# Shifting the stationary split weights by 64 bytes in their buffers

## The chip, the cores and the metric

The kernel runs on one core of a Trainium2 chip. The metric is the device time of one execution in microseconds (us); the kernel before took 1667.27 us as the median of three executions (1665.71 to 1668.77).

## The reference

Two transformer-like blocks run one after the other on 256 tokens of width 1024, all in 32-bit floats. The first has a gated feed-forward layer, a mixer (a chunked mLSTM and a spatial gating unit) and a second feed-forward layer. The second block has two rounds of feed-forward, mixer (a pooled state-space layer in the first round, latent attention in the second), feed-forward, each modulated by vectors computed from `c`. Nearly all of the work is products of the tokens with large weight matrices, above all the six feed-forward layers:

```python
def swiglu(x, w_in, w_out):
    gate, up = jnp.split(x @ w_in, 2, axis=-1)     # w_in: 1024 x 5632
    return (jax.nn.silu(gate) * up) @ w_out        # w_out: 2816 x 1024
```

## The kernel before

Every large product is computed in three passes of a fast 32-bit mode (the type `F32R`). An operand `a` is split into `hi`, its rounded value, and `lo = a - hi`; `mm3` (L503 to L507) then adds `hi*hi`, `hi*lo` and `lo*hi` into the same PSUM tile, one matmul on each of the lines L505, L506 and L507. A matmul has a stationary operand of 128 columns, which a weight load puts into the array first, and a moving operand that streams through it column by column.

The weights arrive from HBM in 1 MB pieces (`raw`), packed in the order of use. A piece holds two units. `_split_one` (L333) turns one unit, 128 partitions by up to 1024 numbers, into a buffer `[P, 2, D]` with `hi` in its first and `lo` in its second half: ScalarE writes `hi` (L352), VectorE writes `lo` (L353). Six such buffers (`sp`) rotate, and between stages up to six working slots (`sx`) are lent to the same purpose; in one stage a pair of other tiles serves (`sg`). `pump` splits ahead as buffers come free, `take` hands out the next unit, `free` gives its buffer back one step later. The order of all units is fixed in the plans at the top of the file (`STAGES`).

A unit is a tuple; the sixth entry of a `cols` unit is the number of 128-row blocks in it. It is 8 for units made by `_mtile` (128 output columns, all of the 1024 input rows) and 2 for units made by `_chunk`. The two kinds are used differently:

- Units with 8 are stationary. `chan_chunk` (L875, chunks 2 to 10 of each feed-forward layer) and `m_tile` (L953, in the two mixers `mix` and `ssd`) take `hi[:, k*128:(k+1)*128]` as the stationary operand and `xh[:, k]` or `xl[:, k]`, the 256 tokens of one 128-row block of the split activations, as the moving one. Each unit makes 8 x 3 = 24 matmuls of 256 columns. There are 6 x 9 x 4 = 216 such units in the feed-forward layers, 16 in `mix` and 12 in `ssd`.
- All other units are moving: 128 tokens of split activations (`xh`, `xl`, `hT` and others) are stationary, and 512 columns (in `mla` also 384 or 288) of `hi` or `lo` stream past them.

`skinny` (L961) makes two small projections whose split weights lie in a tile of their own, `skw`, with 8 (`mix`) or 16 (`ssd`) columns for each 128-row block. There the stationary operand has only those 8 or 16 columns, and the moving one is again `xh[:, k]` or `xl[:, k]`.

The change moves tiles. Within a partition the program before puts the scratch area for DMA descriptors at byte 0 (16384 bytes), `skw` at 25408, `maskb` at 29888, the six `sp` buffers at 54976 and every 8192 bytes after, the eight slots from 104128 on (slots 2 and 5 are 8448 bytes long, the others 8192), and `xh` and `xl` at 170176 and 178368. A 128-column block of a split unit is 512 bytes, a block of `xh` 1024 bytes. So `sp`, all slots, `xh` and `xl` start at the same place in 128 bytes and in 256 bytes; in 512 bytes, slots 3 to 5 start 256 bytes away from the others.

Of the kernel before, what the change touches and what calls it, by code (L numbers as in the profile page):

```python
# [8 lines left out]
F32R = mybir.dt.float32r  # L9
# [4 lines left out]
P = 128  # L14
D = 1024
# [5 lines left out]
LN_EPS = 1e-5  # L21
ROPE_THETA = 10000.0
NEG = -1.0e30

# [88 lines left out]
def _size(u):  # L115
    return D if u[0] == "rows" else u[5] * sum(b - a for a, b in u[3])
# [94 lines left out]
def constants():  # L211
    ident = np.eye(P, dtype=np.float32)
    tri = np.triu(np.ones((P, P), np.float32))
    neg = np.triu(np.full((P, P), NEG, np.float32), 1)
    inv = (ROPE_THETA ** (-np.arange(0, 32, 2, dtype=np.float64) / 32)).astype(np.float32)
# [13 lines left out]
class Builder:  # L229
# [103 lines left out]
    def _split_one(self):  # L333
        u = self.next_split
        gi, base, last = self.group_of[u]
        while self.next_raw <= gi:
            self._load_raw()
        n = _size(self.units[u])
        src = self.raws[gi][:, base:base + n]
        if self.main_free:  # L340
            self.main_free -= 1
            self.where[u] = None
            t = self.p_split.tile([P, 2, D], F32R, tag="sp", name="sp")
        else:
            w = self.extra_free.pop(0)
            self.where[u] = w
            t = self.slot(w, [P, 2, D], F32R, "sx") if w < 8 else None
        if t is None:
            hi, lo = (self.p_gate.tile([P, D], F32R, tag="gate", name="sg") for _ in range(2))
        else:  # L350
            hi, lo = t[:, 0], t[:, 1]
        self.nc.scalar.activation(out=hi[:, 0:n], in_=src, func=AF.Copy)  # L352
        self.nc.vector.tensor_tensor(out=lo[:, 0:n], in0=src, in1=hi[:, 0:n], op=ALU.subtract)  # L353
        self.ready[u] = (hi, lo)
        self.next_split += 1
        if last:
            del self.raws[gi]
            while self.next_raw < len(self.offs) and len(self.raws) < self.RAW_BUFS:
                self._load_raw()
# [1505 lines left out]
```

## Time and profile before

| | |
|---|---|
| median of three executions | 1667.27 us |
| the profiled execution's own time | 1665.83 us |
| its span, first to last instruction | 1664.0 us |
| TensorE matmuls, busy | 1627.7 us (98%), 10290 instructions |
| VectorE, busy | 1180.4 us (71%) |
| ScalarE, busy | 820.9 us (49%) |
| DMA, mean | 219 GB/s |

The profile is of one execution. Its engines are PE (TensorE's matmuls), PEld (its weight loads, which run beside matmuls), DVE (VectorE), ACT (ScalarE), POOL (GpSimd) and SP (the queue that issues most DMAs). A matmul's time in the profile runs from its start to the modelled end of its last result, and matmuls overlap; how fast they follow each other is read from the difference of two starts in the timeline.

### The profile page before, as it was taken

How to read it: one execution, taken by the hardware profiler on the slowest of the kernel's cores; microseconds unless marked ns; L12 is line 12 of the kernel's file. 1: busy time of each engine (PE TensorE's matmuls, PEld its weight loads, DVE VectorE, ACT ScalarE, POOL GpSimd, SP SyncE). 2: the span in 40 equal slices, each digit the busy share in tenths (PEclk: the TensorE clock that was granted, in tenths of full speed). 3: DMA queues.
4: the chain of work that ended last, by engine and by line, in shares of the span. 5: the costliest groups of instructions: out<-in, count | busy, mean ns of one | idle time of the engine just before them, and what ended most of it. 6: DMA issues, size and time to landing. Idle time of an engine off the chain costs nothing.

```text
span 1664.0 us, 25287 instructions
## 1 busy us (share of the span) xinstructions
PE 1627.7 (98%) x10290; PEld 1462.1 (88%) x10290; DVE 1180.4 (71%) x1729; ACT 820.9 (49%) x1161; POOL 53.1 (3%) x81
## 2 busy tenths in 40 slices
PE   8999999999999999999999999999999999999997
PEld 6999889888799988999898789998999987889997
DVE  6698578796687867777586777766777576676553
ACT  6544465445554446444465464444544366555442
POOL 0000001100000000000004000000000010000000
PEclk9999999999999999999999999999999999999999
DMA  8788354676588745887344269873788444147640
GB/s 315 263 326 326 124 189 148 231 251 213 199 301 285 288 154 220 313 296 284 108 150 148 101 253 335 289 285 117 283 298 289 144 166 152 52 177 255 226 164 26
DMA packets 62469, 363.80 MB, mean 219 GB/s; under 512 B 7056, under 2 KB 7184, under 8 KB 28944
## 3 DMA queue, kind: packets, MB, share of 16 engines
q1 hardware_dynamic: 62208, 362.10, 60.3%
q8 instruction: 81, 1.33, 0.3%
q14 instruction: 36, 0.29, 0.1%
q10 hardware_dynamic: 144, 0.08, 0.0%
HBM read 361.11 MB, written 1.05 MB: 218 GB/s over the span
## 4 chain that ended last, share of the span: by engine, by line
PE 89%; DVE 5%; ACT 4%; DMA 1%; issue 1%; POOL 0%; POOLq 0%; SPq 0%; ACTq 0%; DVEq 0%
PE tp L506 14%; PE tp L507 14%; PE tp L505 14%; PE mm L505 7%; PE mm L507 7%; PE mm L506 7%; PE mm L690 7%; PE mm L691 7%; PE mm L697 7%; DVE sp L353 2%; DMA raw<-in_wts 1%; ACT sp L352 1%; ACT xn L635 1%; PE tp L618 1%; ACT xn L586 1%
## 5 line engine op out<-in xcount | busy, mean ns | idle before, releaser
L353 DVE TENSOR_TENSOR sp<-raw,sp 128x1024 fp32r<-128x1024 f32 (+2 forms) x375 | 453.5, 1220 | 224.8 <-ACT sp L352 224.4
L352 ACT ACTIVATE sp<-raw 128x1024 fp32r<-128x1024 f32 (+2 forms) x375 | 389.7, 1050 | 388.9 <-PE tp L507 212.2
L505 PE MATMUL tp<-xh,sp 128*128 128x256 f32 x1032 | 292.5, 283 | 0.2 <-ACT gate L463 0.2
L506 PE MATMUL tp<-xl,sp 128*128 128x256 f32 x1032 | 292.0, 283 | 0.0
L507 PE MATMUL tp<-xh,sp 128*128 128x256 f32 x1032 | 292.0, 283 | 0.0
L353 DVE TENSOR_TENSOR sx<-raw,sx 128x1024 fp32r<-128x1024 f32 x161 | 196.2, 1221 | 97.2 <-ACT sx L352 96.8
L352 ACT ACTIVATE sx<-raw 128x1024 fp32r<-128x1024 f32 x161 | 169.3, 1054 | 177.6 <-PE tp L507 125.7
L505 PEld LDWEIGHTS tp<-xh,sp 128*128 128x128 f32 x1032 | 198.0, 192 | 1.4 <-ACT gate L463 0.5
L506 PEld LDWEIGHTS tp<-xl,sp 128*128 128x128 f32 x1032 | 198.0, 192 | 0.9
L505 PE MATMUL tp<-xh,sx 128*128 128x256 f32 x696 | 197.2, 283 | 0.8 <-ACT gate L463 0.8
L507 PEld LDWEIGHTS tp<-xh,sp 128*128 128x128 f32 x1032 | 198.0, 192 | 0.0
L507 PE MATMUL tp<-xh,sx 128*128 128x256 f32 x696 | 196.9, 283 | 0.0
L506 PE MATMUL tp<-xl,sx 128*128 128x256 f32 x696 | 196.9, 283 | 0.0
L427 DVE SCALAR_TENSOR_TENSOR mraw<-mraw,c_act 128x1024 f32<-128x1024 f32 x144 | 175.3, 1218 | 0.0
L505 PEld LDWEIGHTS tp<-xh,sx 128*128 128x128 f32 x696 | 133.5, 192 | 1.9 <-ACT gate L463 1.0
L505 PE MATMUL mm<-sp,xh 128*128 128x512 f32 (+2 forms) x340 | 133.0, 391 | 1.8 <-ACT xh L639 1.8
L506 PEld LDWEIGHTS tp<-xl,sx 128*128 128x128 f32 x696 | 133.5, 192 | 0.9
L507 PEld LDWEIGHTS tp<-xh,sx 128*128 128x128 f32 x696 | 133.5, 192 | 0.0
L507 PE MATMUL mm<-sp,xl 128*128 128x512 f32 (+2 forms) x340 | 130.0, 382 | 0.2
L506 PE MATMUL mm<-sp,xh 128*128 128x512 f32 (+2 forms) x340 | 129.5, 381 | 0.0
L690 PE MATMUL mm<-sp,hT 128*128 128x512 f32 x246 | 96.6, 393 | 2.6 <-ACT hT L864 2.0
L691 PE MATMUL mm<-sp,hT 128*128 128x512 f32 x246 | 96.2, 391 | 0.0
(472 smaller groups left out, 2796.0 us busy)
## 6 DMA issues: line engine op xcount, KB each, us to landing
raw<-in_wts SPq DMA_DIRECT2D x260, 1024.0 KB, 5.2
mraw<-in_mod SPq DMA_DIRECT2D x144, 512.0 KB, 5.5
raw<-in_wts SPq DMA_DIRECT2D x4, 768.0 KB, 4.5
raw<-in_wts SPq DMA_DIRECT2D x5, 512.0 KB, 5.1
row<-in_rows SPq DMA_DIRECT2D x3, 512.0 KB, 6.3
raw<-in_wts SPq DMA_DIRECT2D x2, 576.0 KB, 4.1
rows<-in_rows SPq DMA_DIRECT2D x2, 512.0 KB, 6.4
bp<-in_pool SPq DMA_DIRECT2D x1, 1024.0 KB, 7.7
```

The lines of the kernel that those rows point to most:

```text
L352: self.nc.scalar.activation(out=hi[:, 0:n], in_=src, func=AF.Copy)
L353: self.nc.vector.tensor_tensor(out=lo[:, 0:n], in0=src, in1=hi[:, 0:n], op=ALU.subtract)
L427: nc.vector.scalar_tensor_tensor(out=src, in0=src, scalar=1.0, in1=self.c_act, op0=ALU.mult, op1=ALU.mult, accum_out=acc[:, kt:kt + 1])
L505: nc.tensor.matmul(out, ah, bh, start=first, stop=False)
L506: nc.tensor.matmul(out, ah, bl, start=False, stop=False)
L507: nc.tensor.matmul(out, al, bh, start=False, stop=last)
L586: nc.scalar.activation(out=xn[:, sl], in_=x[:, sl], func=AF.Square, scale=1.0 / 32.0, accum_out=ss[:, h:h + 1])
L618: nc.tensor.transpose(ps[:, j, :], src[:, k * P:(k + 1) * P], self.ident)
L635: nc.scalar.activation(out=vb[1][:, j], in_=banks[1][:, j], func=AF.Identity, scale=g[:, 4 + j:5 + j], bias=sh[:, 4 + j:5 + j])
L690: nc.tensor.matmul(accs[t][h], ah, hi[:, sl], start=(k == 0), stop=False)
L691: nc.tensor.matmul(accs[t][h], ah, lo[:, sl], start=False, stop=False)
L697: nc.tensor.matmul(accs[t][h], al, hi[:, sl], start=False, stop=False)
```

## The change

A split buffer becomes `[P, 2, D + 64]`, 256 bytes longer in each half, 8704 bytes in all. Units with 8 blocks, the stationary ones, are written and read 16 numbers (64 bytes) further into each half; all other units stay at the start of each half. The second half (`lo`) of every unit starts 4352 bytes after the first instead of 4096. The slots 3, 4, 6 and 7 grow by 512 bytes, 2 and 5 by 256. The scratch area for DMA descriptors that the program reserves goes from 16384 to 2048 bytes, and everything behind it moves down.

```diff
+DP = D + 64
+SHIFT = 16
...
-            t = self.p_split.tile([P, 2, D], F32R, tag="sp", name="sp")
+            t = self.p_split.tile([P, 2, DP], F32R, tag="sp", name="sp")
...
-            t = self.slot(w, [P, 2, D], F32R, "sx") if w < 8 else None
+            t = self.slot(w, [P, 2, DP], F32R, "sx") if w < 8 else None
...
-            hi, lo = t[:, 0], t[:, 1]
+            o = SHIFT if self.units[u][0] == "cols" and self.units[u][5] == 8 else 0
+            hi, lo = t[:, 0, o:o + D], t[:, 1, o:o + D]
...
-    nc = bacc.Bacc("TRN2", target_bir_lowering=False, num_devices=1)
+    nc = bacc.Bacc("TRN2", target_bir_lowering=False, num_devices=1, dynamic_dma_scratch_size=2048)
```

## Rows read from the trace of the kernel before

**Rows 1.** The page: span, busy time of the engines, granted clock and DMA in 40 slices.

```profile
span 1664.0 us, 25287 instructions
...
PE 1627.7 (98%) x10290; PEld 1462.1 (88%) x10290; DVE 1180.4 (71%) x1729; ACT 820.9 (49%) x1161; POOL 53.1 (3%) x81
...
PEclk9999999999999999999999999999999999999999
...
GB/s 315 263 326 326 124 189 148 231 251 213 199 301 285 288 154 220 313 296 284 108 150 148 101 253 335 289 285 117 283 298 289 144 166 152 52 177 255 226 164 26
```

**Rows 2.** The page: the chain that ended last, by engine.

```profile
PE 89%; DVE 5%; ACT 4%; DMA 1%; issue 1%; POOL 0%; POOLq 0%; SPq 0%; ACTq 0%; DVEq 0%
```

**Rows 3.** Groups by line and shape, TensorE: count, busy us, mean ns, idle before.

```profile
L505 PE MATMUL tp<-xh,sp 128*128 128x256 f32 x1032 | 292.5, 283 | 0.2 <-ACT gate L463 0.2
...
L505 PE MATMUL tp<-xh,sx 128*128 128x256 f32 x696 | 197.2, 283 | 0.8 <-ACT gate L463 0.8
...
L505 PE MATMUL mm<-xh,sp 128*128 128x256 f32 x224 | 64.8, 289 | 0.0
```

**Rows 4.** TensorE's timeline, first feed-forward layer, one chunk: start us, us, instruction.

```profile
58.27 0.28 PE L505 MATMUL tp<-xh,sp 128*128 128x256 f32 x1
58.38 0.28 PE L506 MATMUL tp<-xl,sp 128*128 128x256 f32 x1
...
69.78 0.40 PE L690 MATMUL mm<-sx,hT 128*128 128x512 f32 x1
...
75.25 0.28 PE L505 MATMUL tp<-xh,sp 128*128 128x256 f32 x1
```

**Rows 5.** TensorE's timeline, the projection with 8 stationary columns.

```profile
215.50 0.28 PE L505 MATMUL tp<-xh,skw 128*8 128x256 f32 x1
...
217.02 0.28 PE L506 MATMUL tp<-xl,skw 128*8 128x256 f32 x1
...
217.49 0.28 PE L507 MATMUL tp<-xh,skw 128*8 128x256 f32 x1
...
218.28 0.40 PE L505 MATMUL mm<-sp,xh 128*128 128x512 f32 x1
```

**Rows 6.** TensorE's timeline, the projection with 16 stationary columns.

```profile
827.18 0.28 PE L505 MATMUL tp<-xh,skw 128*16 128x256 f32 x1
...
829.99 0.28 PE L505 MATMUL mm<-xh,sp 128*128 128x256 f32 x1
```

**Rows 7.** TensorE's timeline, 288 moving columns of a split unit.

```profile
1359.54 0.29 PE L505 MATMUL mm<-sp,xh 128*128 128x288 f32 x1
...
1359.94 0.30 PE L505 MATMUL mm<-sp,xh 128*128 128x288 f32 x1
...
1360.34 0.29 PE L505 MATMUL mm<-sp,xh 128*128 128x288 f32 x1
```

**Rows 8.** TensorE's timeline, plain 32-bit matmuls and the 512-column ones behind them.

```profile
300.00 1.02 PE L1071 MATMUL tp<-qT,kT 128*128 128x256 f32 x4
300.86 0.61 PE L1073 MATMUL tp<-qT,kT 128*128 128x128 f32 x4
...
301.54 0.40 PE L506 MATMUL mm<-sp,xh 128*128 128x512 f32 x1
...
302.47 0.39 PE L507 MATMUL mm<-sp,xl 128*128 128x512 f32 x1
```

**Rows 9.** TensorE's timeline, the first matmuls after a stall.

```profile
173.72 0.28 PE L506 MATMUL tp<-xl,sx 128*128 128x256 f32 x1
...
174.78 0.28 PE L506 MATMUL tp<-xl,sx 128*128 128x256 f32 x1
```

**Rows 10.** Busy time by window, first feed-forward layer: engines, granted clock, DMA share, GB/s.

```profile
40.00:174.00 134.00, 133.19 (x957) 126.09 (x956) 107.05 (x133) 62.42 (x70) 0.00 (x0) 1.00 0.83 307
```

**Rows 11.** The page's groups, ScalarE's half of the split: busy, mean ns, idle before, releaser.

```profile
L352 ACT ACTIVATE sp<-raw 128x1024 fp32r<-128x1024 f32 (+2 forms) x375 | 389.7, 1050 | 388.9 <-PE tp L507 212.2
...
L352 ACT ACTIVATE sx<-raw 128x1024 fp32r<-128x1024 f32 x161 | 169.3, 1054 | 177.6 <-PE tp L507 125.7
```

## The prediction

> **What bounds the kernel now.** I read the page first: TensorE is busy for 1627.7 of 1664.0 us, at a granted clock of 9 or more tenths in every slice, the 2.4 GHz level [rows 1]. The chain that ended last agrees, 89% of it TensorE [rows 2]. The other engines follow: the ScalarE half of the split spends its idle time waiting for TensorE's matmuls of line L507 to give a buffer back [rows 11], not the other way round. So time is won or lost in the pace of matmuls, and a cheaper VectorE or DMA would bring nothing.
>
> Next, the groups by shape. The matmuls that the change shifts are those with `sp` or `sx` as stationary and 256 columns of `xh` or `xl` as moving operand. Line L505 alone has 1032 + 696 + 224 = 1952 of them [rows 3]; L506 and L507 have as many each, in all 5856, which is also what the plans give (244 units x 24). Their mean of 283 ns is start to end and says nothing of the pace, so I took the pace from the timeline. In one chunk of the first feed-forward layer, 96 of them run from 58.27 to 69.78 us, 11.51 us or 119.9 ns each [rows 4]. At 2.4 GHz 256 columns are 106.7 ns, so each carries 13.2 ns, 32 columns' worth, beyond its stream. Over 5856 that is 77 us, 4.6% of the span: all that the change can possibly win there.
>
> **The change part by part.** *No instruction is added or removed.* The splits keep their shapes, the DMAs their sizes and order. The writes of a split land elsewhere. ScalarE's split takes 1050 ns into `sp` and 1054 ns into `sx` [rows 11], tiles at quite different addresses, so I cost the moved writes at nothing. If they did grow by a tenth, the cover would be the waiting on TensorE in the same rows: 388.9 us before 389.7 us of work on ScalarE.
>
> *The DMA scratch.* 14336 bytes go, and 6 x 512 + 2560 = 5632 bytes are needed. All packets that carry weights are issued from SP in the kernel's code. I cost the smaller area at nothing; the cover, if it delayed descriptors, is the prefetch of three raw pieces. It would show first in the first feed-forward layer, which already moves 307 GB/s [rows 10].
>
> *The address arithmetic.* Everything behind the scratch moves by 14336 and then by 5632 bytes, both multiples of 256. So in 256 bytes all tiles keep their places, and the one new thing is that 5856 matmuls have their stationary operand 64 bytes away from the place of their moving one. Besides, the `lo` halves move by 256 bytes; that this is harmless is shown by `sx`: three of its slots already lie 256 bytes away from `sp`, and their group has the same 283 ns as that of `sp` [rows 3]. A shift by 128 bytes is in the trace too: with 288 moving columns every second block starts 1152 bytes on, 128 beyond a multiple of 256, and one block after the other takes the same 0.40 us for three [rows 7], 133.3 ns each or again 32 columns over the 288. So 128 and 256 bytes make no difference; if an offset matters at all it does so in 128 bytes, where 64 is as far from the present state as one can go.
>
> *What a matmul pays for.* Four rows bracket it. Plain 32-bit matmuls with 256 columns follow each other in 0.86 us / 4 = 215 ns [rows 8]; if I read the doubled pace as two passes of 106.7 ns, about 2 ns are left, so a matmul with a full stationary operand need not carry 13 ns. With only 8 stationary columns against the same moving tile the pace is 1.52 us / 13 = 116.9 ns at first and 0.79 us / 7 = 112.9 ns at the end [rows 5]; with 16 it is 2.81 us / 24 = 117.1 ns [rows 6]. And full-width ones after a stall, started in another rhythm against their weight loads, take 1.06 us / 9 = 117.8 ns [rows 9]; the first after a 512-column one takes 0.11 us [rows 4]. So the 13 ns are not a constant of the mode: they shrink when the weight load reads little, and change with the rhythm between load and stream. That looks like the load's reads and the stream's reads meeting in the same part of the memory, and in the steady state both begin at the same place in 128 bytes.
>
> *The value taken.* Ends: nothing (119.9 ns stays) and the plain 32-bit remainder (106.7 + 2 = 109 ns). Between them I take 113 ns, the pace of the narrow load at the end of rows 5 and of the first matmul in rows 4; nearest in kind, since stream and mode are the same and only the meeting is missing. That is 6.9 ns x 5856 = 40.4 us. I take a tenth off, 4 us, because runs that start after a stall already go at 118 [rows 9] and because the supply gets tighter: a chunk and its two output units take 16.98 us now (58.27 to 75.25 [rows 4]), 0.66 us less then, so 307 GB/s become 319 against 335 in the fastest slice [rows 1, 10], and VectorE's 107.05 of 134.00 us become 83% [rows 10]. Both still fit. Sum: 40.4 - 4 = 36 us, 1665.83 - 36 = 1630 us against the profiled execution's own time. That execution is 1.4 us under the median of 1667.27; I leave 1630.
>
> The Trainium skill, "TensorE: Matmul & The Clock Gate", section "Wait — 56ns, not 53.3ns?", gives back-to-back matmuls as N / 2.4 GHz plus about 2.5 ns. That is 109.2 ns for 256 columns, which this trace does not reach (119.9); by it the whole excess would be avoidable, (119.9 - 109.2) x 5856 = 63 us, an estimate of 1603.
>
> **The rivals.** *The address does not matter.* The 32 columns are what a weight load costs in this mode wherever its operand lies. For it: the same 32 columns or so stand over 256, over 288 and over 512 columns, whose 24 matmuls in this chunk take 5.47 us, 228 ns each against a stream of 213 [rows 4, 7]; and with 16 stationary columns, whose blocks step by 64 bytes, the pace is 117.1 ns throughout with no sign of two kinds [rows 6]. Against it: the pace after a stall and the 112.9 ns of rows 5, which need no other length of load than the 116.9 ns before them. Time: 1666, within 0.2%.
>
> The Trainium skill speaks for this rival: "SBUF — State Buffer", section "Who interferes with whom", says that TensorE has two independent read ports, for the stream and for the load, and waits for nobody. By that rule no placement of operands changes the pace and the time stays at 1666; rows 5 and 9 agree with it only if the rhythm of issue alone makes their difference.
>
> *Only the steady rhythm is broken.* The shift ends the exact 119.9 ns and gives the 117 to 118 ns of rows 6 and 9: 2 to 3 ns x 5856 = 12 to 18 us, 1648 to 1654.
>
> *Slower.* The new offset puts load and stream into a worse rhythm instead. The trace has one: 512-column matmuls right after plain 32-bit ones take 0.93 us / 4 = 232.5 ns [rows 8] against 228 in the chunk of rows 4. The same 5 ns on 5856 matmuls is 29 us, 1695. It decides from 0.6 ns each (3.3 us). Against it: neither of the two runs of 256-column ones that I timed is above 120 ns [rows 4, 9].
>
> **How the numbers follow.** About 0.2%, 3.3 us, can be told from no change. Chances: 0.38 for the forecast's 113 ns, 0.08 for nearly all of the excess (about 1603), 0.14 for the weak gain (1648 to 1654), 0.25 for no change (1663 to 1669), 0.15 for slower. I lean to a gain because one offset class alone is in the trace for full loads and its cost varies without it. Faster is thus 0.60, same 0.25, slower 0.15. The likeliest is 1630, its own range 1620 to 1640. The range that leaves out the slower case and little below goes from 1603 to 1669.
>
> **What would show it.** The start-to-start pace of the 96 matmuls of a chunk: 113 ns, 10.85 us instead of 11.51, if right; 11.51 again for the first rival; 11.3 for the weak gain; over 11.55 for slower. The 512-column matmuls should keep 228 ns, splits 1.05 us. If the pace falls and the span does not follow, TensorE must wait for `sp` on L505 or for raw pieces in the first layer. The prediction is wrong if the pace of 119.9 does not move, or if it falls well under 113.

## The result, and the profile after

The changed kernel takes 1649.95 us, the median of four executions (1648.23 to 1652.19), against 1666.79 us for the kernel before measured beside it. The ratio is 0.9898 with a 95% interval of 0.9881 to 0.9916: 1.0% faster. I had forecast 1630; the direction held, the size did not. 1650 is inside the stretch in which the rival "only the steady rhythm is broken" stood (1648 to 1654).

The page after gives the same number of instructions and, within 0.4 us, the same busy times of all engines but TensorE's; its matmuls, its weight loads and the span lose nearly 16 us each [rows 1].

```profile
span 1648.3 us, 25287 instructions
...
PE 1612.2 (98%) x10290; PEld 1446.2 (88%) x10290; DVE 1180.0 (72%) x1729; ACT 821.1 (50%) x1161; POOL 53.2 (3%) x81
```

The lines of the file are five further on: L510, L511 and L512 are the three passes, L357 the ScalarE half of the split. Its groups on the page have the same means, 1050 and 1055 ns [rows 11], so the moved writes cost nothing, and still TensorE is waited for:

```profile
L357 ACT ACTIVATE sp<-raw 128x1024 fp32r<-128x1024 f32 (+2 forms) x375 | 390.0, 1050 | 378.9 <-PE tp L512 202.8
...
L357 ACT ACTIVATE sx<-raw 128x1024 fp32r<-128x1024 f32 x161 | 169.4, 1055 | 172.5 <-PE tp L512 121.6
```

The timeline of TensorE over a chunk of the first feed-forward layer (start us, us, instruction) is what the prediction said to look at:

```profile
76.41 0.28 PE L510 MATMUL tp<-xh,sp 128*128 128x256 f32 x1
...
87.71 0.40 PE L695 MATMUL mm<-sp,hT 128*128 128x512 f32 x1
...
93.18 0.28 PE L510 MATMUL tp<-xh,sx 128*128 128x256 f32 x1
```

The 96 matmuls take 11.30 us, 117.7 ns each, where they took 119.9 [rows 4]. The 24 of 512 columns behind them take 5.47 us as before. But another stretch of the same timeline, the last chunk of that layer, has another pace:

```profile
173.64 0.28 PE L511 MATMUL tp<-xl,sx 128*128 128x256 f32 x1
...
173.99 0.28 PE L511 MATMUL tp<-xl,sx 128*128 128x256 f32 x1
...
184.42 0.40 PE L695 MATMUL mm<-sp,hT 128*128 128x512 f32 x1
```

It begins behind eight plain 32-bit transposes and a stall of 0.81 us, as the run of [rows 9] did. There the pace was 117.8 ns over the first nine matmuls. Here it falls, and the 92 matmuls from 173.99 us on take 10.43 us, 113.4 ns each: the pace that I had forecast for all. So with 64 bytes between the operands there are two steady rhythms, 117.7 and 113.4 ns, and most runs are in the slow one. (A run is an unbroken sequence of these 256-column matmuls.)

The weight loads tell the two apart. In the trace before, those of the 96 matmuls take 192 ns on all three lines. In the change, at the pace of 117.7 ns (77 to 87 us), they take 192 ns on one line and 188 on the other two; at 113.4 ns (175 to 184 us), 188 on all three (groups of PEld: count, busy us, mean ns, idle before):

```profile
L512 PEld LDWEIGHTS tp<-xh,sp 128*128 128x128 f32 x21 | 3.9, 188 | 0.0
L510 PEld LDWEIGHTS tp<-xh,sp 128*128 128x128 f32 x21 | 3.9, 188 | 0.0
L511 PEld LDWEIGHTS tp<-xl,sp 128*128 128x128 f32 x20 | 3.8, 192 | 0.0
...
L510 PEld LDWEIGHTS tp<-xh,sp 128*128 128x128 f32 x24 | 4.5, 188 | 0.0
L512 PEld LDWEIGHTS tp<-xh,sp 128*128 128x128 f32 x23 | 4.3, 188 | 0.0
L511 PEld LDWEIGHTS tp<-xl,sp 128*128 128x128 f32 x23 | 4.3, 188 | 0.0
```

The other long runs of the change agree. It goes with the pace here; it is not shown to set it.

Summed over the starts of all 5856 such matmuls in the two traces, the 75 runs of them take 705.1 us before and 688.3 us after, 120.4 and 117.5 ns each. The 16.8 us between them are a little more than the 15.7 us by which the two spans differ (1664.0 and 1648.3), so these matmuls are the whole of the gain, and about 1 us was lost elsewhere.

The supply has kept up in the first feed-forward layer. In the same window as [rows 10] TensorE is busy for the same 133.19 of 134.00 us, the rest being the stall above, and the DMAs move 310 GB/s instead of 307 (window: busy us of PE, PEld, DVE, ACT and POOL, granted clock, DMA share, GB/s):

```profile
40.00:174.00 134.00, 133.19 (x965) 125.76 (x965) 107.10 (x134) 62.75 (x70) 0.00 (x0) 1.00 0.85 310
```

### The profile page after: what moved, and what is told of

Same layout as the page of the kernel before. It is cut to its first block, busy times and chain, and to the rows that moved or that the text cites. A ratio compares the mean times of both kernels' runs of the same rounds, so it can differ in the third digit from the quotient of the medians.

```text
span 1648.3 us, 25287 instructions
## 1 busy us (share of the span) xinstructions
PE 1612.2 (98%) x10290; PEld 1446.2 (88%) x10290; DVE 1180.0 (72%) x1729; ACT 821.1 (50%) x1161; POOL 53.2 (3%) x81
## 4 chain that ended last, share of the span: by engine, by line
PE 90%; DVE 4%; ACT 4%; issue 1%; DMA 1%; POOL 0%; POOLq 0%; SPq 0%; ACTq 0%; DVEq 0%
PE tp L512 14%; PE tp L510 14%; PE tp L511 14%; PE mm L510 7%; PE mm L512 7%; PE mm L511 7%; PE mm L695 7%; PE mm L696 7%; PE mm L702 7%; DVE sp L358 1%; ACT sp L357 1%; PE tp L623 1%; DMA raw<-in_wts 1%; ACT xn L640 1%; ACT xn L591 1%
## 5 line engine op out<-in xcount | busy, mean ns | idle before, releaser
L357 ACT ACTIVATE sp<-raw 128x1024 fp32r<-128x1024 f32 (+2 forms) x375 | 390.0, 1050 | 378.9 <-PE tp L512 202.8
L510 PE MATMUL tp<-xh,sp 128*128 128x256 f32 x1032 | 289.7, 281 | 0.2 <-ACT gate L468 0.2
L512 PE MATMUL tp<-xh,sp 128*128 128x256 f32 x1032 | 289.1, 280 | 0.0
L511 PE MATMUL tp<-xl,sp 128*128 128x256 f32 x1032 | 289.1, 280 | 0.0
L357 ACT ACTIVATE sx<-raw 128x1024 fp32r<-128x1024 f32 x161 | 169.4, 1055 | 172.5 <-PE tp L512 121.6
L511 PEld LDWEIGHTS tp<-xl,sp 128*128 128x128 f32 x1032 | 197.3, 191 | 0.9
L510 PE MATMUL tp<-xh,sx 128*128 128x256 f32 x696 | 195.8, 281 | 0.8 <-ACT gate L468 0.8
L512 PE MATMUL tp<-xh,sx 128*128 128x256 f32 x696 | 195.4, 281 | 0.0
L511 PE MATMUL tp<-xl,sx 128*128 128x256 f32 x696 | 195.4, 281 | 0.0
L510 PEld LDWEIGHTS tp<-xh,sp 128*128 128x128 f32 x1032 | 193.7, 188 | 1.4 <-ACT gate L468 0.5
L512 PEld LDWEIGHTS tp<-xh,sp 128*128 128x128 f32 x1032 | 193.8, 188 | 0.0
L510 PE MATMUL mm<-sp,xh 128*128 128x512 f32 (+2 forms) x340 | 133.0, 391 | 1.8 <-ACT xh L644 1.8
L511 PEld LDWEIGHTS tp<-xl,sx 128*128 128x128 f32 x696 | 133.3, 192 | 0.9
L510 PEld LDWEIGHTS tp<-xh,sx 128*128 128x128 f32 x696 | 130.6, 188 | 1.9 <-ACT gate L468 1.0
L512 PEld LDWEIGHTS tp<-xh,sx 128*128 128x128 f32 x696 | 130.7, 188 | 0.0
L512 PE MATMUL mm<-sp,xl 128*128 128x512 f32 (+2 forms) x340 | 130.0, 382 | 0.2
L511 PE MATMUL mm<-sp,xh 128*128 128x512 f32 (+2 forms) x340 | 129.4, 381 | 0.0
```

The lines of the kernel that those rows point to most:

```text
L510: nc.tensor.matmul(out, ah, bh, start=first, stop=False)
L511: nc.tensor.matmul(out, ah, bl, start=False, stop=False)
L512: nc.tensor.matmul(out, al, bh, start=False, stop=last)
```

## The experiments

My theory, as it stood after the result, was that the pace of these matmuls depends on the distance between the places of the moving operand and of the weights that are loaded meanwhile (theory A), and that with 64 bytes two rhythms are possible, picked by what ran just before the run (A2). The rivals: other parts of the change are the gain (B); something else in the chunks behind a stall makes them fast (C). All kernels below are the changed one with the edit shown. The fences show the first matmul of one chunk's run of 96 in the first feed-forward layer and the first behind it, from TensorE's timeline.

**The change without its 64 bytes.**

```diff
-SHIFT = 16
+SHIFT = 0
```

> The whole change but with a shift of 0 bytes: longer buffers, the second half 4352 bytes on, the smaller scratch area. Theory A (the 64 bytes between the stationary and the moving operand are the gain): chunks go back to 119.9 ns per 256-column matmul, 1667 us. Theory B (the gain is from the longer buffers, the moved second half or the smaller scratch area): 117.8 ns and 1650 us stay.

Measured: 1667.05 us, ratio to before 1.0003 (0.9994 to 1.0013).

```profile
76.67 0.28 PE L510 MATMUL tp<-xh,sp 128*128 128x256 f32 x1
...
88.18 0.40 PE L695 MATMUL mm<-sp,hT 128*128 128x512 f32 x1
```

11.51 us, 119.9 ns, as in [rows 4]. Theory B falls: longer buffers, the moved second half and the smaller scratch area are worth nothing that could be told apart from zero, in either direction.

**Other distances.** The same edit with 32, 8, 24, 48 and 12 numbers: 128, 32, 96, 192 and 48 bytes.

> The change with a shift of 128 bytes instead of 64. Theory A, with the place counted in 128 bytes: as with a shift of 0, 119.9 ns and 1667 us. If the place is counted in 256 bytes or more: another pace than 119.9 ns, for instance the 117.8 ns and 1650 us of the shift by 64. Theory B: 1650 us.

Measured: 1667.17 us, ratio 1.0007 (0.9997 to 1.0016).

```profile
76.83 0.29 PE L510 MATMUL tp<-xh,sp 128*128 128x256 f32 x1
...
88.35 0.40 PE L695 MATMUL mm<-sp,hT 128*128 128x512 f32 x1
```

11.52 us, 120.0 ns: at 128 bytes the gain is gone. The match with 0 bytes is not perfect: several runs behind plain transposes settle at about 118.7 ns here and at 120.0 with 0 bytes. Over all 5856 matmuls that is 0.5 us (704.6 against 705.1).

> The change with a shift of 32 bytes. Theory A, cost falling smoothly with the distance of the two places: about half of the gain, 118.9 ns and 1659 us. If load and stream only must not begin in the same 32 bytes: as with 64 bytes, 117.8 ns and 1650 us. Theory B: 1650 us.

Measured: 1657.78 us, ratio 0.9950 (0.9935 to 0.9965).

```profile
76.15 0.28 PE L510 MATMUL tp<-xh,sp 128*128 128x256 f32 x1
...
87.51 0.40 PE L695 MATMUL mm<-sp,hT 128*128 128x512 f32 x1
```

11.36 us, 118.3 ns, between the two outcomes; the total is the first one's, about half of the gain.

> The change with a shift of 96 bytes, 32 bytes before the same place in 128. If the distance counts alike in both directions: as the shift by 32 bytes. If the load must run behind or ahead of the stream: another pace than with 32 bytes, since the sign is turned round. Theory B: 1650 us.

Measured: 1652.72 us, ratio 0.9920 (0.9904 to 0.9937).

```profile
75.67 0.28 PE L510 MATMUL tp<-xh,sp 128*128 128x256 f32 x1
...
86.93 0.40 PE L695 MATMUL mm<-sp,hT 128*128 128x512 f32 x1
```

11.26 us, 117.3 ns. That is not the pace of 32 bytes, so the two directions differ. In the usual run, behind 512-column matmuls, 96 bytes are even a little better than 64. The total is not, since no run reaches the fast rhythm: behind plain transposes some go at 118.7 ns instead, so there are two paces with 96 bytes too, and there the usual one is the faster.

> The change with a shift of 192 bytes, 64 bytes before the same place in 256. If the place counts in 128 bytes alone: 117.8 ns behind 512-column matmuls, 113 ns behind a stall, 1650 us, as with 64. If it counts in 256 bytes: another pace.

Measured: 1654.65 us, ratio 0.9923 (0.9907 to 0.9939). Behind 512-column matmuls the pace is 117.8 ns, as with 64 bytes. Behind the stall it is not (matmuls 2 to 96 of that run):

```profile
173.79 0.28 PE L511 MATMUL tp<-xl,sx 128*128 128x256 f32 x1
...
184.98 0.40 PE L695 MATMUL mm<-sp,hT 128*128 128x512 f32 x1
```

11.19 us for 95, 117.8 ns. So the slow rhythm's pace is the same with 64 and with 192 bytes, but the fast one is rare here: of the runs of at least 48 matmuls, only 96 of 5544 matmuls are in runs that go at 116 ns or less on average, against 768 in the change. With the weights 64 bytes behind the moving operand's place (192 is 64 short of 256) it is not quite the same as with 64 bytes ahead. The weight loads take 187 to 189 ns at the pace of 117.8 ns here (78 to 87 us), so a short load alone does not make the fast rhythm.

> The change with a shift of 48 bytes. The shifts so far gave 118.3 ns at 32 bytes, 117.8 or 113.3 at 64 and 117.3 at 96 in steady runs. Theory A2 (the fast rhythm needs the full half of 128 bytes): one rhythm near 118 ns, 1652 to 1658 us. If the fast rhythm has a width: runs at 113 to 114 ns behind a stall or everywhere, 1635 to 1650 us.

Measured: 1656.70 us, ratio 0.9937 (0.9921 to 0.9953). In the same chunk the run goes from 76.72 to 88.08 us, 118.3 ns, and no long run is in the fast rhythm; the first of the two outcomes. Together with 118.3 ns at 32 bytes this speaks against a cost that falls smoothly with the distance.

**The moving operand shifted instead.**

```diff
-SHIFT = 16
+SHIFT = 0
...
-        self.xh = self.p_xT.tile([P, 8, S], F32R, tag="xh", name="xh")
-        self.xl = self.p_xT.tile([P, 8, S], F32R, tag="xl", name="xl")
+        self.xh, self.xl = (self.p_xT.tile([P, 8 * S + 64], F32R, tag=n, name=n)[:, 16:16 + 8 * S].rearrange(
+            "p (k t) -> p k t", k=8) for n in ("xh", "xl"))
```

> Shift of 0 for the weights; instead the split activations xh and xl start 64 bytes further on. Theory A (the distance of the two places counts): the 256-column runs go at 117.8 ns as in the change; the 512-column matmuls that have xh or xl as stationary get the same distance too, so the total is 1650 us or, if they gain as well, down to 1645. If the place of the weights themselves counts: 119.9 ns and 1667 us.

Measured: 1660.00 us, ratio 0.9960 (0.9945 to 0.9975).

```profile
76.48 0.28 PE L510 MATMUL tp<-xh,sp 128*128 128x256 f32 x1
...
87.79 0.40 PE L695 MATMUL mm<-sp,hT 128*128 128x512 f32 x1
...
173.78 0.28 PE L511 MATMUL tp<-xl,sx 128*128 128x256 f32 x1
...
184.98 0.40 PE L695 MATMUL mm<-sp,hT 128*128 128x512 f32 x1
```

The weights lie where they lay before, and yet the run takes 11.31 us, 117.8 ns; behind the stall 11.20 us for 95, 117.9 ns. Here the weights are 64 bytes behind the stream, as in the shift by 192 bytes, and the two kernels agree: all 5856 matmuls take 692.7 and 692.1 us. It is the distance that counts. My total missed for two reasons. The fast rhythm is nearly gone, which costs 4.4 us against the change's 688.3. And the 512-column matmuls with `xh` or `xl` as stationary do not gain from the distance but lose: from one start to the next they take 233.3 instead of 227.7 ns, which lifts the mean of all 512-column ones from 227.9 to 230.1 (steps over 300 ns, the stalls, left out).

**A plain transpose ahead of each run.** An identity is transposed into the tile that the run then overwrites.

```diff
                     hi, lo = self.take()
+                    if o is outs[0] and m == 0:
+                        nc.tensor.transpose(o[:, 0:P], self.ident, self.ident)
```

> The change, and in front of each chunk's run of 96 stationary-weight matmuls one plain 32-bit transpose of the identity into the tile that the run then overwrites. Theory A2 (with 64 bytes there are two steady rhythms, 113.3 ns after plain 32-bit work and 117.8 ns after 512-column matmuls, and the entry picks one): the 54 chunk runs go at 113 to 114.5 ns, 0.3 to 0.4 us less for each and 0.12 to 0.15 us for the transpose: 10 to 15 us less than the change, 1635 to 1640 us. Theory C (the runs at 113 ns owe it to something else in those chunks, not to what ran just before): 117.8 ns stays and the transposes cost 6 to 8 us, 1657 us.

Measured: 1656.03 us, ratio 0.9936 (0.9921 to 0.9950).

```profile
75.63 0.27 PE L887 MATMUL tp<-cst 128*128 128x128 f32 x1
75.66 0.36 PE L510 MATMUL tp<-xh,sp 128*128 128x256 f32 x1
75.86 0.28 PE L511 MATMUL tp<-xl,sp 128*128 128x256 f32 x1
...
87.05 0.39 PE L695 MATMUL mm<-sp,hT 128*128 128x512 f32 x1
```

The 95 matmuls from 75.86 us on take 11.19 us, 117.8 ns. A plain 32-bit matmul directly ahead does not put a run into the fast rhythm. Theory A2 in that form falls, and the time is the one named for theory C. But theory C does not have it all either. In each of the six feed-forward layers one chunk's run is cut in half by transposes of `hbuf`, which stand there in all these kernels. Behind them the second half settles at 113.3 ns in all six layers of the change, and at 117.8 in four of the six here. So neither what stands directly ahead nor the chunk alone picks the rhythm.

The same with a shift of 0:

> The same transposes with a shift of 0. Theory A2: with both operands at the same place there is one steady rhythm, so after some ten matmuls at 118 ns each run is back at 119.9; 5 to 7 us more than before, 1672 to 1674 us. If the transposes alone help: below 1667 us.

Measured: 1673.10 us, ratio 1.0040 (1.0027 to 1.0053), inside the expected stretch. With equal places nothing lasting changes: the long runs settle at 120 ns again, and the 54 transposes cost 6 us.

**All units shifted, the moving ones too.**

```diff
-            o = SHIFT if self.units[u][0] == "cols" and self.units[u][5] == 8 else 0
+            o = SHIFT
```

> All units shifted by 64 bytes, the moving ones too. The 256-column runs keep the change's 117.8 ns. For the 512-column matmuls: if the distance counts for them as well, their 227 ns falls by 2 to 7 ns on some 3100 of them, 6 to 20 us, 1630 to 1644 us; if a 512-column stream outlasts its load and the distance doesn't matter, 1650 us; if the moved stream is worse off, over 1655 us.

Measured: 1638.11 us, ratio 0.9838 (0.9815 to 0.9862), inside the first expected stretch and for another reason than the one expected.

```profile
75.55 0.28 PE L510 MATMUL tp<-xh,sp 128*128 128x256 f32 x1
...
86.46 0.39 PE L695 MATMUL mm<-sp,hT 128*128 128x512 f32 x1
```

The 512-column matmuls got slower, 229.3 ns on average instead of 227.9. The 256-column run, whose own operands lie as far apart as in the change, takes 10.91 us, 113.6 ns: it is in the fast rhythm, where 117.8 ns had been expected. What differs is the place of the moving data in the matmuls around it; the next two kernels ask which of them matter.

**Which units do that.** These two kernels shift a part of the moving units besides the stationary ones: the rows units, whose products with `w_out` (the output products) run directly ahead of the chunk runs, or the two-block units, which run at the start of a stage.

```diff
-            o = SHIFT if self.units[u][0] == "cols" and self.units[u][5] == 8 else 0
+            o = SHIFT if self.units[u][0] == "rows" or self.units[u][5] == 8 else 0
```

> The stationary units and, of the moving ones, only the rows units (the output products, which run directly ahead of the 256-column runs) are shifted by 64 bytes. Theory D (what runs directly ahead picks the rhythm): the 256-column runs of the feed-forward layers go at 113.6 ns as with all units shifted, and the 512-column matmuls with xh or xl as stationary get their 1 to 3 ns back: 1634 to 1638 us. If it needed all units: 117.8 ns, about 1653 us.

Measured: 1637.32 us, ratio 0.9822 (0.9807 to 0.9837).

```profile
75.09 0.28 PE L510 MATMUL tp<-xh,sp 128*128 128x256 f32 x1
...
86.00 0.39 PE L695 MATMUL mm<-sp,hT 128*128 128x512 f32 x1
...
91.49 0.28 PE L510 MATMUL tp<-xh,sx 128*128 128x256 f32 x1
...
711.23 0.28 PE L511 MATMUL tp<-xl,sx 128*128 128x256 f32 x1
...
722.42 0.40 PE L695 MATMUL mm<-sp,hT 128*128 128x512 f32 x1
```

10.91 us, 113.6 ns, at the price of 5.49 instead of 5.47 us for the 24 output matmuls. The last two rows are a run behind plain transposes, and it is slow: 11.19 us for 95, 117.8 ns.

```diff
-            o = SHIFT if self.units[u][0] == "cols" and self.units[u][5] == 8 else 0
+            o = SHIFT if self.units[u][0] == "cols" else 0
```

> The stationary units and only the two-block moving units are shifted by 64 bytes; the rows units stay. Theory D: the matmuls directly ahead of the runs are the change's again, so 117.8 ns in the chunk runs, and a little more for the shifted 512-column ones: 1650 to 1654 us. If the rhythm hangs on the two-block units or on the number of shifted buffers: 113.6 ns and 1638 us.

Measured: 1650.44 us, ratio 0.9904 (0.9885 to 0.9923).

```profile
76.17 0.28 PE L510 MATMUL tp<-xh,sp 128*128 128x256 f32 x1
...
87.48 0.40 PE L695 MATMUL mm<-sp,hT 128*128 128x512 f32 x1
```

11.31 us, 117.8 ns: the slow rhythm. The two kernels together show that it is the shift of the output products' moving operand, and not that of the two-block units, that puts most chunk runs into the fast rhythm. Counting runs of at least 48 matmuls by their average, 768 of 5544 matmuls are in runs at 116 ns or less in the change, 912 with the two-block units shifted and 4032 with the rows units shifted. The last version beats the kernel before by 1.8% and the change by 0.8%; against all units shifted the intervals overlap.

The shifted products directly ahead do not decide alone, though. In two of the six layers of that best version, seven runs with 864 matmuls stay slow behind output products of the same lines with the same shift. The first of them:

```profile
537.20 0.28 PE L510 MATMUL tp<-xh,sx 128*128 128x256 f32 x1
...
548.50 0.40 PE L695 MATMUL mm<-sx,hT 128*128 128x512 f32 x1
```

11.30 us, 117.7 ns. In both layers the slow stretch begins where plain transposes split a chunk's run into 24 and 72 matmuls, and it lasts to the end of the layer.

## Why the prediction was wrong

- *TensorE's pace is the bound; the rest is free.* Right. All of the gain is in the starts of the 5856 matmuls, the other engines' busy times stand, and the scratch, the buffers and the moved second half are worth nothing (1.0003, 0.9994 to 1.0013). The second half's move was taken for harmless from the means of 283 ns in [rows 3], which run from start to end and so cannot show a pace; the control with 0 bytes shows it.
- *The place of stationary against moving operand matters, in 128 bytes.* Right in the main: 128 bytes give 120.0 ns and no gain, 32, 48, 96 and 192 bytes give 118.3, 118.3, 117.3 and 117.8. That it is a distance is shown by moving the other operand. "In 128" is not the whole of it: 64 and 192 bytes are the same place in 128, and the fast rhythm is common with the one and rare with the other. That two reads meet in the memory, the prediction's reason, is not shown by any run.
- *The value taken: 113 ns.* This step failed. The term of 6.9 ns measured 2.9 ns on average (120.4 to 117.5), 16.8 us instead of 40.4. What the runs showed in its place are two steady rhythms, 113.3 and 117.8 ns, and 46 of the 62 runs of at least 48 matmuls come behind 512-column matmuls, where 117.8 is the pace in the change. The 112.9 ns at the end of [rows 5] lies near the one and the 116.9 ns of the same rows near the other; that the narrow loads go in the same two rhythms is not shown. I took the first for the cost with the meeting gone and gave the second, the rival "only the steady rhythm is broken", 0.14. The single step of 0.11 us in [rows 4] stands right behind a 512-column matmul and is not repeated in a run that goes on at 119.9; I read it as a pace. The low end of 109 ns rests on reading a plain 32-bit matmul as two passes, which no run shows; no long run settled below 113.3.
- *A tenth taken off for stalls and supply.* Not borne out. The supply cost nothing: TensorE's idle time in the window of the first layer is the same 0.81 us as before. And runs behind a stall do not "already go at 118": those are the first nine steps of [rows 9] only. The run goes on to its end at 120.0 ns, 10.32 us for the 86 matmuls from 174.78 us to this line of the trace before:

```profile
185.10 0.40 PE L690 MATMUL mm<-sp,hT 128*128 128x512 f32 x1
```

In the change that same run is one of the fastest, not one with less to gain.

- *The rival that the address does not matter.* Excluded by the control with 0 bytes against the change, and by the shift of the moving operand. The Trainium skill, "SBUF — State Buffer", section "Who interferes with whom", has TensorE's two read ports independent and waiting for nobody; these runs do not agree with the time that follows from it, 1666, since moving one of the two operands by 64 bytes takes 2.2 ns off every matmul in the steady run. Whether a port is what waits was not shown by any run.
- *The slower rival.* Its mechanism, a worse rhythm, exists on the other kind of matmul: with `xh` and `xl` moved, the 512-column ones that load them as weights take 233.3 instead of 227.7 ns.
- *The range*, 1603 to 1669, held the time, but it held no change at all too. The forecast gain of 36 us was 2.1 times the measured 16.8.

What stays open: what picks the rhythm. Most runs behind plain transposes went fast in the change, but the one at 1212.70 us went slow. With one transpose added, nearly all chunk runs stayed slow. In the best version four runs behind transposes went slow, three of which had gone fast in the change, and in two layers the slow rhythm then lasted through chunk runs that are fast elsewhere. No run told these apart.

## What to carry to other kernels

In this kernel, buffers of power-of-two size put a matmul's stationary and moving operands at the same place in 128 bytes, and that cost 2.2 to 6.5 ns of 120; where a trace shows such an excess, try a few offsets, in both directions, with a control that keeps the rest of the edit. Then look at what runs ahead: the same kind of run went at 117.7 or at 113.6 ns by the place of other matmuls' data. When the trace of before shows two paces for one kind of work, price a change at both, and give the one that stands behind the usual neighbours the larger chance.

## What the runs showed of the hardware that was not expected

- Two steady paces for matmuls of one shape with the same distance between their operands: 117.7 and 113.4 ns in one execution, over 96 and 92 matmuls. Weight loads take 192 ns on one of three lines at the first pace, 188 ns on all at the second.
- The pace of a run can hang on other matmuls: shifting the moving data of the output products by 64 bytes turned 117.8 into 113.6 ns in most chunk runs, while 864 matmuls behind the same products stayed at 117.8.
- The sign of the distance counts: 96 bytes gave 117.3 ns and 32 bytes 118.3 ns.
- For 512-column matmuls, the places of the kernel before are the best of those tried: 227.9 ns on average, against 229.3 with all moving units and 230.1 with `xh` and `xl` moved by 64 bytes.
